# A weight sum made one product ahead in the first down phase of a hybrid recurrent / gMLP / convolutional-FFN block

## The chip, the cores and the metric

The kernel runs on one core of a Trainium2 chip. Its time is the device time of one execution in microseconds; the median of three runs before the change is 2160.91 us (2159.95 to 2163.38). The engines are TensorE (PE in the rows, its weight loads PEld), VectorE (DVE), ScalarE (ACT), GpSimd (POOL) and SyncE (SP, which here only issues transfers). Sixteen DMA engines move data between HBM and the on-chip memory.

## The reference, cut to what matters

The block takes x of 2048 x 1024 floats. A mixer (a gated linear recurrence and a gMLP side by side) is followed by a feed-forward part, each between two RMS norms with a shift, a scale and a gate worked out from c. The change touches the last product of the feed-forward part alone:

```
h = rmsnorm(x, g_ffn_pre) * (1.0 + sc_f) + sh_f
up = causal_depthwise_conv(h @ w_up, ffn_conv_w, ffn_conv_b)
g_ff, v_ff = split(up, 2)
y = (gelu(g_ff) * v_ff) @ w_down          # 2048 x 3072 by 3072 x 1024
x = x + gt_f * rmsnorm(y, g_ffn_post)
```

Everything is float32. The kernel writes each operand of a matmul as a high part (rounded to the type that TensorE reads) and a low part (the rest), and computes high x high + high x low + low x high: three matmuls for one.

## The kernel before, in words

The positions are worked on in two halves of 1024 (C = 0 and C = 1). After the mixer come four phases: up for C = 0, down for C = 0, up for C = 1, down for C = 1. The last two are the second up phase and the second down phase below.

**A down phase** (`down_fast`) computes g @ w_down by a scheme of the Strassen-Winograd kind: the features are halved into even and odd blocks, the positions and the output columns into halves, and seven products of sums of these quarters take the place of eight of plain quarters. The products run in this order, each named by its left operand and its weight: "11" x "11", "s1" x "t1", "s2" x "t2", "s4" x "22", "s3" x "t3", "12" x "21", "22" x "t4". The left sums s1 to s4 were stored in HBM (gsd) during the up phase. The weights t1 = 12 - 11, t2 = 22 - t1, t3 = 22 - 12 and t4 = 21 - t2 are sums of quarters of w_down. In C = 0 they are made and stored in HBM (wsd), in C = 1 they are loaded from there.

A product has six steps (q = 0 to 5) of 24 matmuls of 128 x 512: two feature blocks, four column blocks, three matmuls each (L1155). Its results gather in four PSUM banks, A or B. A step's operands come from `operands` (L1132 to L1150): the left raw tile is loaded (L1139), cast to its high part by ScalarE (L138), and the low part is a difference on VectorE (L143); the weight likewise. A "t" weight in C = 0 goes through `weight_sum` (L1119 to L1130): it loads both summands, subtracts (L1126), splits, and ScalarE's queue stores the sum (L1129). Between steps, `tick` advances background work. In the first down phase this is `h2_next`, which loads the normed input of the second half (L231, L859, L860) and builds the 28 operand tiles of the second up phase.

**Tiles.** All large tiles are 128 x 1024 floats, 512 KB. They come from four pools: "t4" with 36 (operands of the up phase, results, and here some raw tiles), "w" with 8 (high and low parts), "wraw" with 4 (raw weights), "ld" with 3 (raw loads and the results of the up phase, until these are stored). A pool's tile is given again only when every reader of its last use is done, a store of it included. In the first product, steps 0 and 1 (`first`) take raw tiles and parts from "t4"; the others use "w", "wraw" and, in C = 1, "ld".

**Order.** A planner orders the instructions of each engine and each queue when the kernel is built, by the order in the source and its own estimates of time; `high_priority(offset=n)` moves what stands in its block ahead by n instructions, so that loads and splits run ahead of their use. On the chip each engine and each queue works in that fixed order: a load that must wait for its tile holds back every load behind it in SyncE's queue.

Of the kernel before, what the change touches and what calls it, by code (L numbers as in the profile page):

```python
# [10 lines left out]
F32 = mybir.dt.float32  # L11
F32R = mybir.dt.float32r
AF = mybir.ActivationFunctionType
ALU = mybir.AluOpType

P = 128
# [24 lines left out]
def block_kernel(ctx: ExitStack, tc: tile.TileContext, xt, cols, rows, wada, wada_r, win_k, win_s, win_v, wgate, wsp, wout, wup, wdown, out):  # L41
    nc = tc.nc
    const = ctx.enter_context(tc.tile_pool(name="const", bufs=1))
    tp = hp = ctx.enter_context(tc.tile_pool(name="tp", bufs=36))
    wp = ctx.enter_context(tc.tile_pool(name="wp", bufs=8))
    rw = ctx.enter_context(tc.tile_pool(name="rw", bufs=4))
    lp = ctx.enter_context(tc.tile_pool(name="lp", bufs=3))
# [6 lines left out]
    vec, act, pool, pe, sync = nc.vector, nc.scalar, nc.gpsimd, nc.tensor, nc.sync  # L54

    def t4(name):
        return tp.tile([P, 2, 512], F32, tag="t4", name=name)
# [4 lines left out]
    def h4(name):  # L62
        return hp.tile([P, 2, 512], F32R, tag="t4", name=name)
# [37 lines left out]
    def wait(n):  # L101
        for _ in range(n):
            yield
# [32 lines left out]
    def split(hi, lo, src, eng, leng=None):  # L136
        if eng == "act":
            act.copy(out=hi, in_=src)  # L138
        elif eng == "pool":
            pool.tensor_scalar(out=hi, in0=src, scalar1=1.0, scalar2=0.0, op0=ALU.mult, op1=ALU.add)  # L140
        else:
            vec.tensor_copy(out=hi, in_=src)
        (leng or vec).tensor_tensor(out=lo, in0=src, in1=hi.bitcast(F32), op=ALU.subtract)  # L143

    def weight(src, shape, name, eng="act", leng=None, mk=None, ahead=200, mkraw=None):
        with tc.high_priority(offset=ahead):
            raw = mkraw(f"{name}_r") if mkraw else rw.tile(shape, F32, tag="wraw", name=f"{name}_r")
            sync.dma_start(out=raw, in_=src)
            if mk is None:
                hi = wp.tile(shape, F32R, tag="w", name=f"{name}_h")  # L150
                lo = wp.tile(shape, F32R, tag="w", name=f"{name}_l")
            else:
                hi, lo = mk(shape, f"{name}_h"), mk(shape, f"{name}_l")
            split(hi, lo, raw, eng, leng)
        return hi, lo
# [35 lines left out]
    def rms_split(ssum, name, n=512):  # L191
        with tc.high_priority(offset=100):
            shl = y4(f"{name}_hl")
            split(shl[:, 0, :n], shl[:, 1, :n], ssum, "dve")
        return shl
# [358 lines left out]
    def mixer_out(c, late=False):  # L554
        Yt = Y[c]
        O = []
        q = SumSq(f"rp{c}")
        for j in range(4):
            pt = psum(f"o{c}_{j}")
            for b in range(2):  # L560
                wh, wl = weight_once(("o", 2 * j + b), wout[2 * j + b], [P, 8, P], f"wout{c}_{j}_{b}", pool if b else vec)
                for k in range(8):
                    mm3(pt[:, b], (wh[:, k], wl[:, k]), (Yt[k // 2][0][:, k % 2], Yt[k // 2][1][:, k % 2]), k == 0, k == 7)
                tick()
            o = t4(f"oo{c}_{j}")
            with tc.high_priority(offset=60 if late else 0):
                act.copy(out=o, in_=pt)
            q.add(o)
            if late:
                sync.dma_start(out=o2d[c - 2, :, j], in_=o)  # L570
            else:
                O.append(o)
        return O, q
# [233 lines left out]
    for j in range(2):  # L807
        a = t4(f"xc0_{j}")
# [11 lines left out]
    for c in range(1, NC):  # L820
# [8 lines left out]
        if c + 1 < NC:  # L829
            ht = start(h_task(c + 1, False), norm_scale(c, 3))  # L830
            O, q = mixer_out(c - 1)
# [39 lines left out]
    def h2_sums(C, i, get, plain=()):  # L871

        a21 = get(1, i, "21")
        a22 = get(1, i + 2, "22")
        if plain:
            put(C, i, "22", a22)
        else:
            a12 = get(0, i + 2, "12", True)
        yield
        vec.tensor_tensor(out=a22, in0=a22, in1=a21, op=ALU.add)  # L880
        put(C, i, "s1", a22)
        yield
        a11 = get(0, i, "11")
        if plain:
            put(C, i, "11", a11)
        yield
        vec.tensor_tensor(out=a22, in0=a22, in1=a11, op=ALU.subtract)
        put(C, i, "s2", a22)
        yield
        vec.tensor_tensor(out=a11, in0=a11, in1=a21, op=ALU.subtract)  # L890
        put(C, i, "s3", a11)
        yield
        if plain:
            a12 = get(0, i + 2, "12")
            put(C, i, "12", a12)
            yield
        vec.tensor_tensor(out=a12, in0=a12, in1=a22, op=ALU.subtract)
        put(C, i, "s4", a12)
# [9 lines left out]
    def from_x2(C, i):  # L908
        return lambda t, j, o: normed(C, t, j, f"xf{C}{i}{o}")
# [187 lines left out]
    def down_fast(C):  # L1097
# [2 lines left out]

        HT = 512

        def a_src(op, q):
            if op[0] == "s":
                i, h = {"s2": (0, 0), "s3": (0, 1), "s4": (1, 0), "s1": (1, 1)}[op]
                return gsd[C, :, 2 * q:2 * q + 2, i, h]
            i, h = {"11": (0, 0), "12": (1, 0), "22": (1, 1)}[op]
            g = gd[C, :, 4 * q:4 * q + 4, HT * h:HT * h + HT]
            return g.rearrange("p (a b) t -> p a b t", b=2)[:, :, i]

        def w_src(k, q):
            if k[0] == "t":
                i, h = {"t1": (0, 0), "t3": (0, 1), "t4": (1, 0), "t2": (1, 1)}[k]
                w = wsd[2 * q:2 * q + 2, i]
            else:
                i, h = {"11": (0, 0), "12": (0, 1), "21": (1, 0), "22": (1, 1)}[k]
                w = wdown[4 * q:4 * q + 4].rearrange("(a b) p d c -> a b p d c", b=2)[:, i]
            return w.rearrange("a p d c -> p a d c")[:, :, 4 * h:4 * h + 4]

        def weight_sum(k, q, name):  # L1120

            a, b = {"t1": ("12", "11"), "t2": ("22", "t1"), "t3": ("22", "12"), "t4": ("21", "t2")}[k]
            raw, other = [rw.tile([P, 2, 4, P], F32, tag="wraw", name=f"{name}_{x}") for x in "ro"]
            sync.dma_start(out=raw, in_=w_src(a, q))
            sync.dma_start(out=other, in_=w_src(b, q))
            vec.tensor_tensor(out=raw, in0=raw, in1=other, op=ALU.subtract)  # L1126
            hl = [wp.tile([P, 2, 4, P], F32R, tag="w", name=f"{name}_{x}") for x in "hl"]
            split(hl[0], hl[1], raw, "act")
            act.dma_start(out=w_src(k, q), in_=raw)  # L1129
            return hl  # L1130

        def operands(op, k, q):  # L1132
            with tc.high_priority(offset=150):
                n = f"{op}_{q}"
                n = f"{C}{op}_{q}"
                first = op == "11" and q < 2
                mk = h_like if first else None
                raw = t4(f"dgr{n}") if first or C == 0 else lp.tile([P, 2, 512], F32, tag="ld", name=f"dgr{n}")
                sync.dma_start(out=raw, in_=a_src(op, q))  # L1139
                if C == 0 and not first:  # L1140
                    g = [wp.tile([P, 2, 512], F32R, tag="w", name=f"dg{x}{n}") for x in "hl"]
                else:
                    g = h4(f"dgh{n}"), h4(f"dgl{n}")
                split(g[0], g[1], raw, "act")
                mkraw = (lambda m: tp.tile([P, 2, 4, P], F32, tag="t4", name=m)) if first else None
                if C == 0 and k[0] == "t":
                    w = weight_sum(k, q, f"dw{n}")
                else:
                    w = weight(w_src(k, q), [P, 2, 4, P], f"dw{n}", ahead=0, mkraw=mkraw, mk=mk)
            return g, w  # L1150

        def mm(pt, g, w, a, d, first, stop):
# [91 lines left out]
        hl = rms_split(acc[1], "fr11")  # L1244
# [27 lines left out]
    def h2_next():  # L1272

        for i in range(2):
            yield from wait(4)
            g = h2_sums(1, i, from_x2(1, i), True)
            for _ in g:
                yield from wait(2)
# [5 lines left out]
    O, q = mixer_out(NC - 2, True)  # L1284
# [13 lines left out]
    up_phase(0, PLAIN, lambda f: start(late_chunks()) if f == PLAIN + 1 else None)  # L1298
    drain()
    start(h2_next())  # L1300
    down_fast(0)
    drain()
    up_phase(1, 0, lambda f: start(first_finals()) if f == 1 else None)
    drain()
    down_fast(1)
    drain()

# [69 lines left out]
```

## Time and profile before

| | |
|---|---|
| median of three runs | 2160.91 us |
| the profiled execution, its own time | 2167.42 us |
| its span, first to last instruction | 2165.6 us |
| TensorE busy | 2014.3 us (93%) |
| VectorE busy | 1553.9 us (72%) |
| ScalarE busy | 953.6 us (44%) |
| GpSimd busy | 440.0 us (20%) |
| moved by DMA | 572.46 MB, mean 264 GB/s |
| first down phase | 1170.8 to 1435.7 us |
| second down phase | 1895.7 to 2141.0 us |

Matmuls overlap: one lasts 0.39 us in the rows, and the next starts 0.23 us after it. A stretch in which TensorE is busy throughout is therefore the measure, not the sum of durations. The granted clock is the share of TensorE's 2.4 GHz that the chip gave over a stretch; it has two levels, full and half. A row of busy time by stretch gives the stretch, its length, then for PE, PEld, DVE, ACT and POOL the busy us and the instructions, then the granted clock, the busy share of the DMA engines and their GB/s. A row with [t <- X] says that the engine stood idle for t us before the instruction, and that X ended the wait.

### The profile page before, as it was taken

What the parts mean: (1) busy time and instruction counts of PE and PEld (TensorE: products, weight loads), DVE (VectorE), ACT (ScalarE), POOL (GpSimd) and SP (SyncE); (2) the same over time, 40 slices, a digit from 0 to 9 for tenths busy, and PEclk for the clock granted to TensorE, in tenths of its full rate; (3) what the DMA queues carried; (4) which work ended last, traced back from release to release, by engine and by line L of the source; (5) the groups of instructions that cost most, each with busy time, mean ns of one, the idle gap of its engine ahead of it and who ended that gap; (6) DMA issues with size and microseconds to landing.
All of it is one profiled execution on the core that took longest, in us unless ns stands there. A gap on an engine that the chain in (4) does not pass through costs nothing.

```text
span 2165.6 us, 23968 instructions
## 1 busy us (share of the span) xinstructions
PE 2014.3 (93%) x8744; PEld 1649.3 (76%) x8744; DVE 1553.9 (72%) x1727; ACT 953.6 (44%) x1226; POOL 440.0 (20%) x250
## 2 busy tenths in 40 slices
PE   5898979999998999999998989999999999979995
PEld 3686868878877887787776777788888888868884
DVE  6787698697576698998897867665555776554557
ACT  3463642633644554454554544443323333343432
POOL 3355243333212234425331000020000000000000
PEclk9898989999999999999999999999999999999997
DMA  8487578677585579889787888867776997666545
GB/s 323 165 311 274 194 261 288 241 261 280 188 300 205 222 284 336 318 321 352 268 314 275 318 301 286 285 237 272 271 280 233 342 358 277 220 203 214 194 148 154
DMA packets 198823, 572.46 MB, mean 264 GB/s; under 512 B 17456, under 2 KB 17584, under 8 KB 198704
## 3 DMA queue, kind: packets, MB, share of 16 engines
q1 hardware_dynamic: 183568, 527.93, 68.5%
q0 software_dynamic: 7456, 26.22, 3.3%
q10 hardware_dynamic: 7680, 16.78, 2.0%
q8 instruction: 69, 1.13, 0.2%
q14 instruction: 50, 0.41, 0.1%
HBM read 372.67 MB, written 199.23 MB: 264 GB/s over the span
## 4 chain that ended last, share of the span: by engine, by line
PE 62%; DVE 17%; DMA 10%; issue 5%; ACT 4%; POOL 1%; SPq 0%; DVEq 0%; ACTq 0%; POOLq 0%
PE dA L1155 9%; PE upa L980 6%; PE upa L982 6%; PE upa L981 6%; PE dB L1155 5%; PE upc L980 3%; PE upc L981 3%; PE upc L982 3%; DVE a L929 2%; PE upb L982 1%; PE upb L981 1%; PE upb L980 1%; DMA dw0s_o<-in_wdown_dram 1%; PE lg L179 1%; PE lg L180 1%
## 5 line engine op out<-in xcount | busy, mean ns | idle before, releaser
L929 DVE SCALAR_TENSOR_TENSOR a<-Rg,prm,a 128x1023 f32<-128x1023 f32 x92 | 127.0, 1381 | 72.8 <-ACT a L927 72.7
L929 DVE SCALAR_TENSOR_TENSOR a<-Rv,prm,a 128x1023 f32<-128x1023 f32 x92 | 139.2, 1513 | 20.7 <-ACT a L927 20.3
L960 POOL TENSOR_TENSOR wug<-wuv,wug 128x512 f32<-128x512 f32 x24 | 46.9, 1954 | 506.5 <-DMA wsd<-dw_r 285.5
L1090 POOL DMA_DIRECT2D out_dram<-do x2 | 2.5, 1342 | 703.0 <-DVE do L1088 703.0
L927 ACT ACTIVATE a<-Rv,prm 128x1024 f32<-128x1024 f32 x46 | 57.2, 1244 | 142.0 <-DVE Rv L1047 141.9
L138 ACT CAST wt<-wug 128x512 fp32r<-128x512 f32 x72 | 44.7, 621 | 114.2 <-POOL wug L964 51.2
L1155 PE MATMUL dA<-dgh,dw_h 128*128 128x512 f32 x192 | 73.5, 408 | 21.2 <-ACT dw_h L138 21.2
L143 DVE TENSOR_TENSOR wt<-wug,wt 128x512 fp32r<-128x512 f32 x72 | 67.8, 942 | 30.7 <-ACT wt L138 30.5
L985 ACT ACTIVATE a<-a 128x1024 f32<-128x1024 f32 x48 | 50.9, 1060 | 86.8 <-DVE a L934 45.4
L1155 PE MATMUL dA<-dgl,dw_h 128*128 128x512 f32 x192 | 73.5, 403 | 0.2 <-DVE dgl L143 0.2
L1155 PE MATMUL dA<-dgh,dw_l 128*128 128x512 f32 x192 | 68.2, 391 | 0.5 <-DVE dw_l L143 0.5
L280 DVE SCALAR_TENSOR_TENSOR ada_m<-wada,cact,ada_m 128x1024 f32<-128x1024 f32 x28 | 45.1, 1612 | 29.2 <-DMA wada<-in_wada_r_dram 29.2
L143 DVE TENSOR_TENSOR dw_l<-dw_r,dw_h 128x1024 fp32r<-128x1024 f32 x36 | 43.9, 1220 | 29.0 <-ACT dw_h L138 28.8
L988 DVE TENSOR_TENSOR gg<-a,a 128x1024 f32<-128x1024 f32 x48 | 58.4, 1216 | 5.8 <-ACT a L985 5.7
L143 DVE TENSOR_TENSOR dgl<-dgr,dgh 128x1024 fp32r<-128x1024 f32 x36 | 43.9, 1222 | 24.5 <-ACT dgh L138 24.2
L1155 PEld LDWEIGHTS dA<-dgh,dw_h 128*128 128x128 f32 x192 | 37.5, 196 | 31.4 <-ACT dw_h L138 23.7
L138 ACT CAST dgh<-dgr 128x1024 fp32r<-128x1024 f32 x36 | 37.7, 1047 | 53.0 <-DMA dgr<-gd 22.6
L143 DVE TENSOR_TENSOR dw1s_l<-dw1s_r,dw1s_h 128x1024 fp32r<-128x1024 f32 x24 | 29.3, 1222 | 42.4 <-ACT dw1s_h L138 42.4
L927 ACT ACTIVATE a<-Rg,prm 128x1024 f32<-128x1024 f32 x46 | 57.1, 1242 | 1.2
L138 ACT CAST dw_h<-dw_r 128x1024 fp32r<-128x1024 f32 x36 | 37.7, 1047 | 39.7 <-PE dA L1155 12.2
L222 POOL TENSOR_TENSOR rp_s<-rp_s,rp_s 128x1024 f32<-128x1024 f32 x12 | 31.3, 2606 | 117.0 <-ACT rp_s L218 116.8
L1051 ACT COPY Rg<-upa 128x512 f32<-128x512 f32 x46 | 26.8, 583 | 55.9 <-PE upa L982 55.9
(651 smaller groups left out, 6885.4 us busy)
## 6 DMA issues: line engine op xcount, KB each, us to landing
wkd<-wt SPq DMA_DIRECT2D x88, 512.0 KB, 3.8
wkd<-w SPq DMA_DIRECT2D x66, 512.0 KB, 5.0
w<-wkd SPq DMA_DIRECT2D x66, 512.0 KB, 4.3
gd<-gg SPq DMA_DIRECT2D x48, 512.0 KB, 5.5
gsd<-gg SPq DMA_DIRECT2D x48, 512.0 KB, 4.1
wrt<-wkd SPq DMA_DIRECT2D x44, 512.0 KB, 4.4
wt<-wkd SPq DMA_DIRECT2D x44, 512.0 KB, 4.9
dgr<-gd SPq DMA_DIRECT2D x36, 512.0 KB, 5.0
```

The lines of the kernel that those rows point to most:

```text
L138: act.copy(out=hi, in_=src)
L143: (leng or vec).tensor_tensor(out=lo, in0=src, in1=hi.bitcast(F32), op=ALU.subtract)
L280: vec.scalar_tensor_tensor(out=flat, in0=w, scalar=cact[:, kt:kt + 1], in1=flat, op0=ALU.mult, op1=ALU.add)
L927: act.activation(out=a, in_=R, func=AF.Identity, scale=w[2], bias=col("ffn_conv_b", blk))
L929: vec.scalar_tensor_tensor(out=a[:, s:], in0=R[:, :FT - s], scalar=w[t], in1=a[:, s:], op0=ALU.mult, op1=ALU.add)
L960: pool.tensor_tensor(out=b11, in0=b12, in1=b11, op=ALU.subtract)
L980: pe.matmul(out=pt, lhsT=wh, rhs=mh, start=first and not more and k == 0, stop=False, skip_group_check=more)
L981: pe.matmul(out=pt, lhsT=wh, rhs=ml, start=False, stop=False, skip_group_check=more)
L982: pe.matmul(out=pt, lhsT=wl, rhs=mh, start=False, stop=last and k == 3, skip_group_check=more)
L985: act.activation(out=g, in_=g, func=AF.Gelu_apprx_tanh)
L988: vec.tensor_tensor(out=flat, in0=g, in1=v, op=ALU.mult)
L1155: pe.matmul(out=pt, lhsT=x[:, a, d], rhs=y[:, a], start=first and z == 0, stop=stop and z == 2, skip_group_check=True)
```

## The change

In the first down phase a weight sum is no longer made in the step that uses it. `AHEAD` names, for four products, the sum that is made while they run: t1 in "11", t2 in "s1", t4 in "s2", t3 in "s4". One of the two summands is the raw weight that the product loads for itself anyway. The new `made` loads the other one into a tile of "t4", subtracts on VectorE, and GpSimd's queue stores the result to wsd. A "t" weight is then loaded from wsd like any other weight, in both halves. Second, the first two steps of both down phases lose their tiles of "t4": the left raw tile comes from "wraw" (C = 0) or "ld" (C = 1), the raw weight from "wraw", the parts of the weight from "w", and in C = 0 those of the left operand too. Third, the background work of the first down phase starts four ticks later.

```diff
+        AHEAD = {"11": [("t1", "12", False)], "s1": [("t2", "22", False)], "s2": [("t4", "21", False)], "s4": [("t3", "12", True)]}
...
-        def weight_sum(k, q, name):
-
-            a, b = {"t1": ("12", "11"), "t2": ("22", "t1"), "t3": ("22", "12"), "t4": ("21", "t2")}[k]
-            raw, other = [rw.tile([P, 2, 4, P], F32, tag="wraw", name=f"{name}_{x}") for x in "ro"]
-            sync.dma_start(out=raw, in_=w_src(a, q))
-            sync.dma_start(out=other, in_=w_src(b, q))
-            vec.tensor_tensor(out=raw, in0=raw, in1=other, op=ALU.subtract)
-            hl = [wp.tile([P, 2, 4, P], F32R, tag="w", name=f"{name}_{x}") for x in "hl"]
-            split(hl[0], hl[1], raw, "act")
-            act.dma_start(out=w_src(k, q), in_=raw)
-            return hl
+        def made(src, q, key, raw, first, name):
+
+            load, store = (a_src, a_src) if key[0] == "s" else (w_src, w_src)
+            other = tp.tile(list(raw.shape), F32, tag="t4", name=name)
+            sync.dma_start(out=other, in_=load(src, q))
+            a, b = (raw, other) if first else (other, raw)
+            vec.tensor_tensor(out=other, in0=a, in1=b, op=ALU.subtract)
+            pool.dma_start(out=store(key, q), in_=other)
 
         def operands(op, k, q):
             with tc.high_priority(offset=150):
-                n = f"{op}_{q}"
                 n = f"{C}{op}_{q}"
-                first = op == "11" and q < 2
-                mk = h_like if first else None
-                raw = t4(f"dgr{n}") if first or C == 0 else lp.tile([P, 2, 512], F32, tag="ld", name=f"dgr{n}")
+                if C == 0:
+                    raw = (rw.tile([P, 2, 512], F32, tag="wraw", name=f"dgr{n}") if op == "11" and q < 2 else t4(f"dgr{n}"))
+                else:
+                    raw = lp.tile([P, 2, 512], F32, tag="ld", name=f"dgr{n}")
                 sync.dma_start(out=raw, in_=a_src(op, q))
-                if C == 0 and not first:
+                if C == 0:
                     g = [wp.tile([P, 2, 512], F32R, tag="w", name=f"dg{x}{n}") for x in "hl"]
                 else:
                     g = h4(f"dgh{n}"), h4(f"dgl{n}")
                 split(g[0], g[1], raw, "act")
-                mkraw = (lambda m: tp.tile([P, 2, 4, P], F32, tag="t4", name=m)) if first else None
-                if C == 0 and k[0] == "t":
-                    w = weight_sum(k, q, f"dw{n}")
-                else:
-                    w = weight(w_src(k, q), [P, 2, 4, P], f"dw{n}", ahead=0, mkraw=mkraw, mk=mk)
+                wraw = rw.tile([P, 2, 4, P], F32, tag="wraw", name=f"dwr{n}")
+                w = weight(w_src(k, q), [P, 2, 4, P], f"dw{n}", ahead=0, mkraw=lambda m: wraw)
+            if C == 0 and op in AHEAD:
+                with tc.high_priority(offset=100):
+                    for key, src, first in AHEAD[op]:
+                        made(src, q, key, raw if key[0] == "s" else wraw, first, f"mk{key}_{q}")
             return g, w
...
     def h2_next():
 
         for i in range(2):
-            yield from wait(4)
+            yield from wait(4 if i else 8)
             g = h2_sums(1, i, from_x2(1, i), True)
```

## Rows read from the trace of the kernel before

**Rows 1.** The page's first part: busy us, share of the span, instructions.

```profile
PE 2014.3 (93%) x8744; PEld 1649.3 (76%) x8744; DVE 1553.9 (72%) x1727; ACT 953.6 (44%) x1226; POOL 440.0 (20%) x250
```

**Rows 2.** Busy time by stretch, second down phase: products 1, 2.

```profile
1895.70:1943.90 48.20, 36.35 (x146) 29.38 (x146) 24.54 (x25) 17.99 (x20) 0.00 (x0) 0.89 0.65 211
1943.90:1976.60 32.70, 32.70 (x146) 27.11 (x145) 14.34 (x12) 14.31 (x18) 0.00 (x0) 1.00 0.58 193
```

**Rows 3.** The same view, first down phase: products 1 to 7 in order.

```profile
1170.80:1214.20 43.40, 34.95 (x145) 28.20 (x146) 34.41 (x34) 24.38 (x30) 0.00 (x0) 0.92 0.72 245
1214.20:1251.20 37.00, 34.86 (x146) 28.01 (x145) 27.32 (x25) 19.97 (x25) 0.00 (x0) 0.95 0.91 325
1251.20:1294.80 43.60, 37.20 (x144) 29.43 (x143) 26.42 (x24) 18.79 (x23) 0.00 (x0) 0.88 0.85 303
1294.80:1327.70 32.90, 32.90 (x146) 27.05 (x144) 22.29 (x20) 16.14 (x18) 0.00 (x0) 1.00 0.77 257
1327.70:1366.80 39.10, 35.08 (x145) 28.09 (x145) 31.53 (x32) 19.07 (x23) 0.00 (x0) 0.96 0.90 315
1366.80:1400.60 33.80, 33.05 (x146) 27.06 (x145) 21.37 (x22) 14.32 (x17) 0.00 (x0) 1.00 0.79 276
1400.60:1435.70 35.10, 33.52 (x146) 26.81 (x145) 23.17 (x25) 15.33 (x21) 3.30 (x3) 1.00 0.90 310
```

**Rows 4.** Waits, 1165 to 1445 us: who for whom, us in total, times, longest.

```profile
ACT dw0s_h L138 <- DVE dw0s_r L1126: 22.3, 11, 4.1
DVE dw0s_r L1126 <- DMA dw0s_o<-in_wdown_dram: 10.8, 7, 2.9
```

**Rows 5.** Timeline of TensorE, first down phase: the two longest of its waits.

```profile
1177.46 0.80 PE L1155 MATMUL dA<-dgh,dw_h 128*128 128x512 f32 x1 [6.67 <-ACT dw_h L138]
...
1281.78 0.80 PE L1155 MATMUL dA<-dgh0s,dw0s_h 128*128 128x512 f32 x1 [4.08 <-ACT dw0s_h L138]
```

**Rows 6.** Waits of SyncE's queue, 1165 to 1445 us.

```profile
SPq L148 <- DMA wsd<-dw0s_r: 15.5, 4, 6.4
```

**Rows 7.** DMA issues by line: count, KB each, median us to landing; and L1129.

```profile
wsd<-dw0s_r ACTq DMA_DIRECT2D x18, 512.0 KB, 6.2
...
dgr<-gd SPq DMA_DIRECT2D x36, 512.0 KB, 5.0
...
kept_s<-win_l POOLq DMA_DIRECT2D x12, 512.0 KB, 7.4
...
L1129 ACTq DMA_DIRECT2D wsd<-dw0s_r x18: 366/418/467, 1201.7 to 1359.5; - x18
```

**Rows 8.** Groups of instructions, 1165 to 1445 us: busy us, mean ns | idle before.

```profile
L1126 DVE TENSOR_TENSOR dw0s_r<-dw0s_r,dw0s_o 128x1024 f32<-128x1024 f32 x18 | 22.0, 1223 | 20.8 <-DMA dw0s_o<-in_wdown_dram 10.8 <-DMA dw0s_o<-wsd 7.0 <-issue 3.0
...
L138 ACT CAST dgh<-dgr 128x1024 fp32r<-128x1024 f32 x18 | 18.9, 1048 | 37.3 <-PE dB L1155 11.8 <-DVE dw_r L1126 11.1 <-PE dA L1155 7.4
...
L859 DVE SCALAR_TENSOR_TENSOR xf<-xf,sf,rq_r 128x512 f32<-128x512 f32 x16 | 11.3, 747 | 4.5 <-DMA xf<-x2d 4.5
```

**Rows 9.** Busy time by stretch: two with high DMA rates, and the first down phase.

```profile
600.00:620.00 20.00, 20.00 (x90) 16.57 (x89) 18.20 (x16) 8.82 (x10) 5.03 (x2) 1.00 1.03 405
...
1700.00:1800.00 100.00, 100.00 (x442) 82.82 (x442) 73.06 (x96) 34.35 (x41) 0.00 (x0) 1.00 0.97 356
...
1170.80:1435.70 264.90, 241.55 (x1009) 194.65 (x1010) 186.51 (x180) 127.98 (x149) 3.30 (x3) 0.95 0.83 290
```

**Rows 10.** Timelines of TensorE, SyncE's queue, its waits: start of the second down phase.

```profile
1904.10 0.80 PE L1155 MATMUL dA<-dgh,dw_h 128*128 128x512 f32 x1 [8.24 <-ACT dw_h L138]
...
1915.19 0.79 PE L1155 MATMUL dA<-dgh,dw_h 128*128 128x512 f32 x1 [3.60 <-ACT dw_h L138]
...
1897.99 0.36 SPq L148 DMA_DIRECT2D dw1s_r<-wsd  x1
1898.40 0.47 SPq L148 DMA_DIRECT2D dw_r<-in_wdown_dram  x1
...
SPq L148 <- DVE dw_l L143: 13.7, 4, 5.0
```

## The prediction

> **What bounds the kernel now.** I read the busy shares first: TensorE is busy for 93% of the span, every other engine less [rows 1]. So a gain can only come from stretches in which TensorE stands still or runs at its lower clock. Then I cut the two down phases into their products (windows). A product is 144 matmuls on one pair of operands, six steps of 24. In the second phase the second product takes 32.7 us with TensorE never idle [rows 2]; that is the price of a product with nothing in its way, 5.45 us a step. Set against it, the seven products of the first down phase take 43.4, 37.0, 43.6, 32.9, 39.1, 33.8 and 35.1 us [rows 3]: 36.0 us too much in all. The first product of the second phase takes 48.2 us [rows 2], 15.5 us too much. The rest of the second phase has no such loss. The change can therefore give back at most 36.0 + 15.5 = 51.5 us.
>
> What the reader is to see in rows 3: the slow products are those whose weight is a sum, "t1", "t2", "t3", "t4" (37.0, 43.6, 39.1, 35.1 us), and the first one, which starts after the up phase. The two plain ones in between, 32.9 and 33.8 us, lose almost nothing. The granted clock is 0.88 in the worst product and 1.00 in the plain ones, so each stall is paid a second time: the matmuls behind it run at the lower of the two levels (1.2 GHz in place of 2.4).
>
> The waits say what is late in a sum product. ScalarE waits 22.3 us for the difference before it can make the high part of the weight [rows 4], VectorE waits 10.8 us for one of the two summands [rows 4], and TensorE stands, in the worst case 4.08 us, until that high part is there [rows 5]. SyncE's queue waits 15.5 us until the stored sum has left its buffer [rows 6]: both summands come from a pool of four, and the sum keeps its buffer until its store has landed, 6.2 us more [rows 7]. With two tiles a step, only two steps are in flight.
>
> **The change, part by part.**
>
> *The sum leaves the path of its user.* A "t" step of the first phase now loads a finished weight, as a plain step does. The chain load, difference, cast, matmul loses the difference (1.22 us [rows 8]) and the wait for the second summand. In the four-tile pool a step takes one tile in place of two, and no store holds it, so weights can be loaded four steps ahead. By the plain products the four sum products would then cost 32.9 to 33.8 us, and of their excess of 24.0 us (4.3 + 10.9 + 6.4 + 2.4) some 20 to 24 would go, if nothing came in its place.
>
> *The same work moves one product earlier.* Nothing is saved in total: still 24 differences of 1.22 us on VectorE, 24 second operands and 24 stores. But the loads and stores now stand in products 1 to 4 ("11", "s1", "s2", "s4"), four 512 KB transfers a step, while products 5 to 7 keep two. Before, it was products 2, 3, 5 and 7 that had four. VectorE's count first: 3 x 1.22 = 3.7 us a step, and the background that prepares the next up phase adds 16 multiplications of 0.75 [rows 8], 14 low parts and 8 sums of 1.22 us, 39 us over its 28 steps or 1.4 a step. That is 5.1 of 5.45 us. VectorE takes its work in order, so a difference that waits for its second operand holds back the low parts behind it, and TensorE waits for those. Only 0.35 us a step is spare.
>
> DMA next. Four products move 24 x 4 x 0.524 = 50.3 MB, the background 4.2 MB more, and some 2.1 MB is loaded before the start: 52.4 MB. To fit in 4 x 32.7 = 131 us this needs 400 GB/s. The trace reached 405 over 20 us and 356 over the best stretch of 100 us [rows 9]; the sum products of this stage ran at 303 to 325 [rows 3]. So the bounds for the four products are 131 us (400 GB/s) and 181 us (290 GB/s, about the mean of this phase). I take 147 us, 356 GB/s, from the nearest row in which TensorE was busy throughout and the transfers were as large. That leaves 16 us of the excess of the first four products, which is 26.1 us now (10.7 + 4.3 + 10.9 + 0.2). Gain there: 10 us, with ends of 26 and -24.
>
> The Trainium skill, in "DMA: Bandwidth & Descriptors", section "Where 436 GB/s comes from", says that for transfers between HBM and SBUF the HBM side binds at about 358 GB/s. The trace of 405 GB/s over 20 us does not agree; the 356 over 100 us does not contradict it. An estimate by that page would put the four products at 52.4 / 0.358 = 146 us, and the gain at 11 us; by the row of 405 GB/s it would be 26.
>
> *Products 5 to 7* have two transfers a step and no difference. They take 3 x 33 = 99 us by the plain rows, against 39.1 + 33.8 + 35.1 = 108.0 now. Gain 9, with ends of 10 (nothing left) and 3 (some of the output's work was the cause, and it stays).
>
> *The stores move from ScalarE's queue to GpSimd's.* ScalarE is spared 24 issues of about 0.42 us [rows 7], which gains nothing, since it is busy for only 41 to 56% of each product [rows 3]. GpSimd does nothing in products 1 to 6 [rows 3], so a store that waits there for its difference holds back no other work. SyncE's queue issues the second operands among the other loads, some 0.4 us each [rows 10], three a step and so 1.2 of 5.45 us. A store from GpSimd landed after 7.4 us [rows 7] against 6.2 from ScalarE. The sum is loaded again one product (33 us) after it is made, less four steps of loading ahead (22 us): 11 us, of which the store takes 7. That hides it; if it did not, SyncE's queue would stand, and every load behind it with that.
>
> *The first steps use the common raw tiles.* In the second phase the first two steps took their raw tiles and parts from the big pool, which the up phase still fills. TensorE stands 8.24 and then 3.60 us, each time for the high part of the weight [rows 10]. That cast waited for a load issued at 1898.40 us, when TensorE had already run dry; ahead of it in the queue stood the load of a weight for the second product, which waited for its buffer [rows 10]. With common tiles the first weights take the places that those of later steps take now, and are loaded in the order of use. What is late next is the first operand: its raw tile now comes from a pool of three in which the last two results of the up phase still sit, so that loads go one at a time, about 5.0 [rows 7] + 1.05 + 1.22 [rows 8] = 7.3 us against a step of 5.45, for two or three steps. I count 48.2 -> 37 us: a gain of 11. Ends: 15.5 (all of it) and -6 (the stalls stay, and three steps of 1.9 us come on top).
>
> In the first phase the same edit touches the first transition, where TensorE stands 6.67 us [rows 5]; there the operands' parts also go to the common pool of eight, which holds two steps. This is within the 10 us of the first four products. The later start of the background (four steps) costs nothing: it ends in the sixth product, still before the up phase that needs it.
>
> **Sum.** 10 + 9 + 11 = 30 us. The profiled execution took 2167.4 us, so 2137.4 of its kind; the median of the runs is 6.5 us lower, 2160.9, which gives 2131 us. Nothing left of any stall would be 2109.
>
> **Rivals.**
>
> *A. The stall moves to VectorE.* The difference waits for its operand in VectorE's queue, and the low part of the current weight behind it. For it: the waits of 10.8 us and the like [rows 4], and the 0.35 us that VectorE has to spare a step. Against it: the second operand now has a tile of the big pool and can be asked for early. If the 24 differences each cost TensorE 1 us, with the lower clock behind it, the first four products keep all their 26 us; products 5 to 7 and half of the second transition remain, 9 + 5 = 14 us: 2147.
>
> *B. Slower: the crowded stretch is bound by DMA.* Place: products 1 to 4 of the first phase; price: 52.4 MB at the rate the phase has now, 290 GB/s, are 181 us in place of 156.9, a loss of 24, and products 5 to 7 give back 9. With the three-tile pool of the second phase giving nothing, the kernel ends 15 us later: 2176; with 5 of its gain, 2171. It decides from a rate of 52.4 / (264.9 - 99) = 316 GB/s downward, or 296 if the second transition brings its 11 us. For it: 303 to 325 [rows 3] are near that point. Against it: in those rows the engines also waited on each other, and 405 shows more to be had.
>
> *C. The change does not act as told.* The stored sum is not back in time, SyncE stands for it, and the sum products stay as they are; only the second transition gains, and the extra traffic early takes that again: about 2158 to 2163. Against it: the 11 us of slack, and a store from GpSimd that is only 1.2 us slower in the rows. The Trainium skill, in "SBUF — State Buffer", section "SBUF: two separate sides", warns that the descriptors of a DMA issued from GpSimd wait while VectorE runs an operation in a 2-port mode, as a float copy does; the operations of VectorE here mostly have two tensors as inputs, and no row here shows such a wait.
>
> **How the numbers follow.** The forecast 0.60, A 0.22, C 0.06, B 0.12. The likeliest gives 2131, with its own range of 2113 to 2143. The 8 in 10 must take in A and part of C, and the floor of 2109 is hardly reached: 2113 to 2161. A measurement of this kernel can tell 0.2%, 4.3 us, from no change. Faster by more: the forecast, A and a little of C, 0.83; within: most of C, 0.05; slower: B, 0.12.
>
> **What would show it.** Right: the four sum products at 33 to 34 us once they load finished weights, except where they make the next sum; the rate over the first four products between 340 and 400 GB/s; the windows of products 5 to 7 at 33 us with a granted clock of 1.00; the gap before the second down phase under 3 us. Wrong: a low part of the weight as the releaser of TensorE in products 1 to 4 (A); a rate under 316 GB/s there with ScalarE waiting for loads (B); SyncE's queue waiting for the stores of the sums (C); first steps of the second phase that wait for the raw operand longer than now.

## The result and the profile after

The changed kernel takes 2139.21 us (median of four runs, 2137.91 to 2140.90), the kernel before 2162.14 us beside it (four runs): 22.9 us less, a ratio of 0.9886 with a 95% interval of 0.9871 to 0.9900. Forecast were 2131 us and a range of 2113 to 2161. The profiled execution took 2139.98 us (span 2138.2), 27.4 us less than the one of before; some 3 us of that lie ahead of the first down phase, where nothing is changed, and are the difference of two executions. So the sums below are made on the phases.

The first group is busy time by stretch for the seven products of the first down phase, which answers to [rows 3] (columns as there). The planner now starts product 1 before the up phase is over: 24 matmuls of the up phase, 5.4 us, lie in its stretch.

```profile
1162.10:1208.50 46.40, 40.35 (x169) 32.27 (x167) 33.73 (x33) 19.47 (x25) 4.61 (x7) 0.96 0.94 351
1208.50:1248.50 40.00, 35.22 (x145) 28.61 (x146) 32.63 (x30) 19.02 (x23) 5.68 (x8) 0.91 1.04 391
1248.50:1281.40 32.90, 32.90 (x146) 26.95 (x145) 27.71 (x27) 18.95 (x24) 3.16 (x5) 1.00 1.04 385
1281.40:1314.00 32.60, 32.60 (x145) 27.01 (x144) 25.73 (x25) 18.16 (x22) 4.12 (x6) 1.00 1.05 398
1314.00:1348.00 34.00, 33.30 (x146) 26.83 (x145) 26.47 (x29) 18.24 (x22) 0.00 (x0) 1.00 0.61 213
1348.00:1380.80 32.80, 32.80 (x146) 26.94 (x145) 23.05 (x24) 17.02 (x20) 0.00 (x0) 1.00 0.65 226
1380.80:1413.40 32.60, 32.60 (x145) 27.00 (x144) 17.64 (x20) 14.46 (x20) 3.31 (x3) 1.00 0.54 186
...
1170.80:1314.00 143.20, 132.37 (x563) 107.66 (x562) 113.25 (x107) 72.25 (x86) 17.57 (x24) 0.96 1.03 389
```

Products 3 to 7 now run like plain ones. Products 1 to 4 take 151.9 - 5.4 = 146.5 us (before 156.9), products 5 to 7 99.4 (before 108.0). The last row is the crowded stretch as a whole: 389 GB/s over 143 us, 55.7 MB. What is left stands in products 1 and 2, 41.0 and 40.0 us against 32.7. TensorE's waits there, answering to [rows 5], with what went before the one of 4.73 us:

```profile
1181.81 1.20 PE L1155 MATMUL dA<-dgh,dw_h 128*128 128x512 f32 x4 [3.20 <-ACT dw_h L138]
...
1208.55 0.50 PE L1155 MATMUL dB<-dgh0s,dw0s_h 128*128 128x512 f32 x1 [2.46 <-ACT dw0s_h L138]
...
1206.06 0.33 SPq L1003 DMA_DIRECT2D gsd<-gg  x1
...
1207.85 5.71 SPq L148 DMA_DIRECT2D dwr0s<-wsd  x3
1213.64 1.56 SPq L231 DMA_DIRECT2D xf<-x2d  x2
...
1222.05 2.75 DVE L859 SCALAR_TENSOR_TENSOR xf<-xf,sf,rq_r 128x512 f32<-128x512 f32 x4 [4.45 <-DMA xf<-x2d]
...
1222.83 1.39 ACT L860 ACTIVATE xf<-xf,modc 128x512 f32<-128x512 f32 x2 [6.68 <-DVE xf L859]
...
1228.81 1.04 ACT L138 CAST dw0s_h<-dwr0s 128x1024 fp32r<-128x1024 f32 x1
...
1229.90 0.79 PE L1155 MATMUL dB<-dgh0s,dw0s_h 128*128 128x512 f32 x1 [4.73 <-ACT dw0s_h L138]
```

Read from the bottom: TensorE waits for a cast that ScalarE makes at 1228.81. ScalarE had stood 6.68 us for the background (L860), which waited for VectorE (L859), which stood 4.45 us for the background's load (xf). That load was issued at 1213.64, behind three weight loads in SyncE's queue. Before these the queue had stood 10.6 us, until 1206.06, for a store of the up phase (L1003), whose tile VectorE had yet to finish (L1001; the wait is the row of L1003 in the next fence). No run changes that alone, so its share in the stop stays open. The weight itself is not late; the work in front of it is. The waits of the sums in [rows 4] and [rows 6] are gone or small: no row of VectorE waiting for a second operand is left among the longest, and SyncE's queue waits 2.9 us for the stores of the sums.

```profile
ACT xf L860 <- DVE xf L859: 8.8, 2, 6.7
...
SPq L1003 <- DVE gg L1001: 11.9, 2, 10.6
...
SPq L148 <- DMA wsd<-mkt: 2.9, 2, 2.0
```

The second down phase, answering to [rows 2] and [rows 10]: product 1 takes 43.1 us in place of 48.2. The second stop of 3.60 us is gone, the first has only changed its releaser: it now ends with the left operand, no longer with the weight.

```profile
1873.50:1916.60 43.10, 35.12 (x146) 28.81 (x146) 24.45 (x25) 17.95 (x20) 0.00 (x0) 0.88 0.71 244
```

```profile
1869.77 6.31 SPq L148 DMA_DIRECT2D dwr1s<-wsd  x2
1876.17 0.42 SPq L1138 DMA_DIRECT2D dgr<-gd  x1
...
1878.39 1.06 ACT L985 ACTIVATE a<-a 128x1024 f32<-128x1024 f32 x1 [2.95 <-DVE a L934]
1880.43 1.05 ACT L138 CAST dgh<-dgr 128x1024 fp32r<-128x1024 f32 x1 [0.98 <-DMA dgr<-gd]
...
1881.53 2.08 PE L1155 MATMUL dA<-dgh,dw_h 128*128 128x512 f32 x4 [7.98 <-ACT dgh L138]
```

The first left operand is loaded at 1876.17 us, 2.6 us after TensorE ran dry, behind two loads of weights of product 2 (dwr1s) that waited for their tiles: what happened to the first weight in [rows 10] now happens to the left operand. But ScalarE stood only 0.98 us for that load. Until 1879.45 it had the last results of the up phase in front of the cast (L985), and for these it stood 2.95 us for VectorE. Before the change it was the same, with 1.27 us for the load of the weight:

```profile
1900.67 1.06 ACT L985 ACTIVATE a<-a 128x1024 f32<-128x1024 f32 x1 [1.99 <-DVE a L934]
1903.00 1.04 ACT L138 CAST dw_h<-dw_r 128x1024 fp32r<-128x1024 f32 x1 [1.27 <-DMA dw_r<-in_wdown_dram]
```

### The profile page after: what moved, and what is told of

Its sections match the earlier page's. It is cut to its first block, busy times and chain, and to the rows that moved or that the text cites. A ratio compares the mean times of both kernels' runs of the same rounds, so it can differ in the third digit from the quotient of the medians.

```text
span 2138.2 us, 24026 instructions
## 1 busy us (share of the span) xinstructions
PE 2006.5 (94%) x8744; PEld 1645.3 (77%) x8744; DVE 1552.7 (73%) x1727; ACT 951.7 (45%) x1226; POOL 457.9 (21%) x274
## 3 DMA queue, kind: packets, MB, share of 16 engines
q10 hardware_dynamic: 1152, 4.19, 0.5%
## 4 chain that ended last, share of the span: by engine, by line
PE 69%; DVE 16%; DMA 5%; issue 5%; ACT 4%; POOL 1%; SPq 0%; DVEq 0%; ACTq 0%; POOLq 0%
PE dA L1155 11%; PE dB L1155 8%; PE upa L980 6%; PE upa L982 6%; PE upa L981 6%; PE upc L981 3%; PE upc L980 3%; PE upc L982 3%; DVE a L929 2%; PE upb L981 1%; PE upb L982 1%; PE upb L980 1%; PE lg L179 1%; PE lg L180 1%; PE lg L181 1%
## 5 line engine op out<-in xcount | busy, mean ns | idle before, releaser
L929 DVE SCALAR_TENSOR_TENSOR a<-Rg,prm,a 128x1023 f32<-128x1023 f32 x92 | 127.0, 1380 | 69.2 <-ACT a L927 69.1
L929 DVE SCALAR_TENSOR_TENSOR a<-Rv,prm,a 128x1023 f32<-128x1023 f32 x92 | 139.2, 1513 | 20.9 <-ACT a L927 20.6
L927 ACT ACTIVATE a<-Rv,prm 128x1024 f32<-128x1024 f32 x46 | 57.2, 1244 | 140.7 <-DVE Rv L1047 140.6
L985 ACT ACTIVATE a<-a 128x1024 f32<-128x1024 f32 x48 | 50.9, 1061 | 88.9 <-DVE a L934 45.4
L1155 PE MATMUL dA<-dgh,dw_h 128*128 128x512 f32 x192 | 69.7, 396 | 11.2 <-ACT dgh L138 8.0
L143 DVE TENSOR_TENSOR dw_l<-dwr,dw_h 128x1024 fp32r<-128x1024 f32 x36 | 43.9, 1220 | 24.7 <-ACT dw_h L138 24.1
L927 ACT ACTIVATE a<-Rg,prm 128x1024 f32<-128x1024 f32 x46 | 57.2, 1242 | 1.3
L143 DVE TENSOR_TENSOR dw1s_l<-dwr1s,dw1s_h 128x1024 fp32r<-128x1024 f32 x24 | 29.3, 1222 | 38.2 <-ACT dw1s_h L138 38.2
L138 ACT CAST dw_h<-dwr 128x1024 fp32r<-128x1024 f32 x36 | 37.8, 1050 | 37.1 <-PE dB L1155 8.7
L1051 ACT COPY Rg<-upa 128x512 f32<-128x512 f32 x46 | 26.9, 584 | 52.5 <-PE upa L982 52.5
```

What stands on the lines that cost most here:

```text
L927: act.activation(out=a, in_=R, func=AF.Identity, scale=w[2], bias=col("ffn_conv_b", blk))
L929: vec.scalar_tensor_tensor(out=a[:, s:], in0=R[:, :FT - s], scalar=w[t], in1=a[:, s:], op0=ALU.mult, op1=ALU.add)
L985: act.activation(out=g, in_=g, func=AF.Gelu_apprx_tanh)
L1155: pe.matmul(out=pt, lhsT=x[:, a, d], rhs=y[:, a], start=first and z == 0, stop=stop and z == 2, skip_group_check=True)
```

## The experiments

Two theories were open after the result. D: in products 1 to 4 the DMA engines are full, and TensorE pays for the bytes. W: the engines and queues stand in their fixed order for other work, the background above all. And the change has three parts, sums ahead (S), first tiles (T) and the later background (B), whose shares a single pair of kernels can't tell. Each ratio below is against the kernel before in the same batch, with its 95% interval. The cuts of code are against the change, in e2 against the kernel before; `...` marks what is left out.

**e1: S and B without T.** The two first steps of product 1 keep their tiles of the big pool, in both halves:

```diff
-                if C == 0:
-                    raw = (rw.tile(...) if op == "11" and q < 2 else t4(f"dgr{n}"))
+                first = op == "11" and q < 2
+                mk = h_like if first else None
+                if C == 0 or first:
+                    raw = t4(f"dgr{n}")
...
-                wraw = rw.tile([P, 2, 4, P], F32, tag="wraw", name=f"dwr{n}")
+                wraw = (tp.tile(...) if first else rw.tile(...))
...
```

> The sums are made one product ahead as in the change, but the first two steps of product 1 keep their tiles of the big pool in both down phases. Theory (the two parts add up: the sums bring about 19 us in the first down phase, the tiles about 5 us at the start of the second): about 2144 us, 18 us under before, and the start of the second down phase stands some 8 and 3.6 us as before. Rival (the tiles also shorten the start of the first down phase, and the sums alone lose there): over 2150.

2155.76 us, ratio 0.9951 (0.9936 to 0.9965). The rival holds: beside the two other parts T is worth 16.6 us in the medians, 14 by the ratios, not 5. The profile shows where: product 1 of the first phase takes 51.9 us, with stops of 6.67 and 7.27 us, and the second phase starts as before (8.41 and 3.25 us). In every kernel here with T the planner starts product 1 before the up phase is over, and the first of these stops is 3.2 us or gone; in the two without T, this one and the kernel before, it starts behind the up phase and stands 6.67.

```profile
1174.98 0.80 PE L1157 MATMUL dA<-dgh,dw_h 128*128 128x512 f32 x1 [6.67 <-ACT dw_h L138]
...
1188.23 1.04 ACT L138 CAST dw_h<-dwr 128x1024 fp32r<-128x1024 f32 x1 [5.73 <-DMA dwr<-in_wdown_dram]
```

**e2: T alone.** The sums stay in `weight_sum`, the background starts after 4 steps.

```diff
-                first = op == "11" and q < 2
-                mk = h_like if first else None
-                raw = t4(f"dgr{n}") if first or C == 0 else lp.tile(...)
+                if C == 0:
+                    raw = (rw.tile(...) if op == "11" and q < 2 else t4(f"dgr{n}"))
+                else:
+                    raw = lp.tile(...)
...
-                    w = weight(w_src(k, q), [P, 2, 4, P], f"dw{n}", ahead=0, mkraw=mkraw, mk=mk)
+                    w = weight(w_src(k, q), [P, 2, 4, P], f"dw{n}", ahead=0)
```

> The first two steps use the common raw tiles in both down phases, the sums stay in the step that uses them, the background starts as before. Theory (parts add up): about 2156 us, 5 us under before, with the sum products at 37 to 43 us as before. Rival (the tiles were what the sums needed; alone they bring nothing or tie up the four raw tiles): 2162 or more.

2165.36 us, ratio 1.0000 (0.9989 to 1.0012): nothing, as the rival said. The second phase gains its 5 us (43.2 us), the first loses 8: one stop of 16.95 us in product 1. Its chain ends as that of the 4.73 us above does: ScalarE stands 17.74 us for the background.

```profile
1203.33 2.74 DVE L859 SCALAR_TENSOR_TENSOR xf<-xf,sf,rq_r 128x512 f32<-128x512 f32 x4 [6.59 <-DMA xf<-x2d]
...
1204.11 1.38 ACT L860 ACTIVATE xf<-xf,modc 128x512 f32<-128x512 f32 x2 [17.74 <-DVE xf L859]
```

**e8: S and T without B.**

```diff
-            yield from wait(4 if i else 8)
+            yield from wait(4)
```

> The change without its third part: the background starts after 4 steps, as before. Theory (the later start is what keeps its loads out of product 1, where ScalarE and VectorE stand in order for them): 5 to 10 us slower than the change, 2144 to 2149. Rival (it matters little where in the full stretch those 4.2 MB lie): 2138 to 2141.

2148.77 us, ratio 0.9929 (0.9905 to 0.9954), 9.6 us over the change's 2139.21. The theory holds. The stop is in product 1, 10.94 us, and the rows are those of W again. The load of the background is issued at 1199.56. In front of it stand three weights that waited 7.6 us for the stores of their sums, and two stores of the up phase's results; for the first of these to land it waited 3.0 us, as both take their tiles from the pool of three (the two rows of the queue's waits, 1180 to 1201 us).

```profile
1185.45 8.30 SPq L148 DMA_DIRECT2D dwr0s<-wsd  x3
...
SPq L148 <- DMA wsd<-mkt: 7.6, 3, 3.7
SPq L231 <- DMA gsd<-gg: 3.7, 2, 3.0
...
1199.56 1.59 SPq L231 DMA_DIRECT2D xf<-x2d  x2
...
1203.50 1.42 DVE L859 SCALAR_TENSOR_TENSOR xf<-xf,sf,rq_r 128x512 f32<-128x512 f32 x2 [7.35 <-DMA xf<-x2d]
...
1204.29 1.38 ACT L860 ACTIVATE xf<-xf,modc 128x512 f32<-128x512 f32 x2 [11.13 <-DVE xf L859]
```

**e9: T and B without S**, which is e2 with

```diff
-            yield from wait(4)
+            yield from wait(4 if i else 8)
```

> The sums stay in the step that uses them; the first steps use the common raw tiles and the background starts after 8 steps in its first half, as in the change. With the tiles alone the first down phase lost 8 us, in one stop of 16.95 us while ScalarE stood for a late load of the background. Theory (that stop is the background's early loads; the later start removes it, the sum products stay slow): 8 to 13 us under the tiles alone, 2152 to 2157. Rival (two summands a step in a pool of four that also holds two left tiles is the cause): 2160 to 2166.

2146.76 us, ratio 0.9931 (0.9912 to 0.9950): the theory in kind, but more than it said, 18.6 us under T alone where 8 to 13 were expected. Beside the change in its own batch (e12) the sums bring 2146.76 - 2140.31 = 6.5 us. Its products show what the sums give and take:

```profile
1159.10:1197.80 38.70, 38.39 (x169) 31.45 (x168) 29.10 (x29) 19.16 (x23) 0.00 (x0) 1.00 0.76 275
1197.80:1236.20 38.40, 33.75 (x146) 26.66 (x144) 30.53 (x29) 22.15 (x28) 0.00 (x0) 1.00 0.98 339
1236.20:1279.40 43.20, 36.28 (x144) 28.77 (x145) 27.78 (x26) 18.71 (x22) 0.00 (x0) 0.92 0.90 313
...
1312.10:1351.60 39.50, 35.31 (x146) 27.85 (x145) 32.71 (x34) 19.54 (x23) 0.00 (x0) 0.96 0.88 311
```

Without the sums ahead, product 1 takes 38.7 - 5.4 = 33.3 us, nearly nothing lost; products 2, 3 and 5 are slow as ever (38.4, 43.2, 39.5). The sums ahead take 15.6 us from products 2 to 7 (220.5 to 204.9) and give 7.7 back in product 1 (33.3 to 41.0).

The length of the first down phase (less the 5.4 us where the up phase reaches into it) and of product 1 of the second puts the parts side by side:

| kernel | first down phase, us | second, product 1, us | median, us |
|---|---|---|---|
| before | 264.9 | 48.2 | 2160.9 to 2164.8 by batch |
| T (e2) | 272.7 | 43.2 | 2165.4 |
| S and B (e1) | 253.4 | 48.3 | 2155.8 |
| S and T (e8) | 256.1 | 43.2 | 2148.8 |
| T and B (e9) | 253.7 | 42.7 | 2146.8 |
| S, T and B: the change | 245.9 | 43.1 | 2139.2 |

Leaving out any one part costs 6.5 to 16.6 us; together these are 32.7, more than the whole gain of 22.9, while T alone brings nothing. The parts lean on each other. S alone and B alone were not run.

**e3: the background later still.**

```diff
-            yield from wait(4 if i else 8)
+            yield from wait(1 if i else 17)
```

> The change, with the background of the first down phase started 9 steps later still (17 in place of 8, and 1 in place of 4 before its second half), so that its loads fall into products 3 to 6. Theory W (what is left in product 2 is ScalarE and VectorE standing in order for a late load of the background): the 4.73 us stop in product 2 and the lower clock behind it go, 7 us, about 2132. Theory D (the DMA engines are full in products 1 to 4 and TensorE loses what the bytes take): 1 to 2 loads, 1 MB, leave product 2 and as much comes to products 3 and 4, which stand then; the sum of products 1 to 4 falls by no more than 3 us unless bytes leave the four products: 2136 to 2140.

2139.22 us, ratio 0.9869 (0.9852 to 0.9887): no change, as D said. The stop of 4.73 us leaves product 2, and one of 3.79 us comes at the start of product 3. The stretches of the four products sum to 151.8 us, in the change to 151.9. That speaks against W's price, not against its mechanism: in front of the cast that ends the new stop ScalarE again works for the background (L860 at 1242.61, then a cast of its tile). The rows of products 2 and 3:

```profile
1209.20:1245.90 36.70, 32.91 (x145) 26.93 (x145) 24.12 (x23) 17.63 (x22) 4.11 (x6) 1.00 1.04 392
1245.90:1281.80 35.90, 34.56 (x144) 28.15 (x145) 27.23 (x24) 14.64 (x16) 5.82 (x8) 0.95 1.02 373
```

**e5 and e6: twelve loads more.** Both add loads that nothing reads, e5 to products 3 and 4, e6 to products 6 and 7:

```diff
+            if C == 0 and op in ("s2", "s4"):        # e6: ("12", "22")
+                with tc.high_priority(offset=100):
+                    extra = t4(f"ex{n}")
+                    sync.dma_start(out=extra, in_=a_src("11", q))
             return g, w
```

> The change, with one load of 512 KB more in each step of products 3 and 4 (12 loads, 6.3 MB; nothing reads them). Theory D (the DMA engines are full there, at some 390 GB/s, and TensorE pays for every byte): 6.3 MB / 0.39 = 16 us more, about 2155, with TensorE standing in products 3 to 5. Theory W (what is left of the stall is the engines' order, the transfers are hidden): 0 to 3 us more, 2139 to 2142.

> The same 12 loads more, now in products 6 and 7, where the change moves 226 and 186 GB/s. Both theories: nothing to pay, 2139 to 2141; over 2145 would mean that not the DMA engines but an issue slot or a tile of the big pool is what an extra load costs, and the run before it could not be read.

e5: 2151.62 us, ratio 0.9941 (0.9919 to 0.9964), 12.4 over the change. e6: 2139.49, ratio 0.9884 (0.9860 to 0.9908), nothing. So an issue and a tile more cost nothing by themselves. In e5 the rate does not rise above the change's 385 and 398; the products get longer instead:

```profile
1246.00:1288.20 42.20, 33.16 (x145) 26.65 (x143) 28.90 (x27) 22.48 (x29) 2.92 (x5) 0.94 1.05 395
1288.20:1324.80 36.60, 35.63 (x144) 28.93 (x145) 25.32 (x24) 15.54 (x18) 4.36 (x6) 0.92 1.05 397
```

6.3 MB at 0.39 MB/us are 16 us; 13.3 us of that are paid in these two products (78.8 against 65.5). D holds for what is added there: the stretch has no room left.

**e7: t4 made in product 6.**

```diff
-        AHEAD = {..., "s2": [("t4", "21", False)], "s4": [("t3", "12", True)]}
+        AHEAD = {..., "s4": [("t3", "12", True)], "12": [("t4", "t2", True)]}
```

> The change, with t4 made in product 6 from its weight 21 and the stored t2, in place of product 3: 6.3 MB leave the crowded products 1 to 4. Theory D: products 2 and 3 and their loads ahead get room, some of the 7 us lost in product 2 comes back, 2133 to 2137; no more, because products 1 and 2 keep their own four transfers a step. Theory W: the stop in product 2 stays, 2139.

2138.42 us, ratio 0.9879 (0.9852 to 0.9906): not told from the change; this one goes to W. Product 2 has become less full (347 GB/s, busy share 0.95), and its stop stays, with ScalarE standing 5.54 us for the background (L860) in front of the cast:

```profile
1208.60:1248.50 39.90, 35.63 (x145) 28.91 (x146) 31.81 (x30) 19.07 (x23) 4.14 (x6) 0.91 0.95 347
...
1229.46 0.79 PE L1155 MATMUL dB<-dgh0s,dw0s_h 128*128 128x512 f32 x1 [4.27 <-ACT dw0s_h L138]
```

**e4: the left tile of the second phase from the four raw tiles.**

```diff
-                if C == 0:
-                    raw = (rw.tile(...) if op == "11" and q < 2 else t4(f"dgr{n}"))
+                if op == "11" and q < 2:
+                    raw = rw.tile(...)
+                elif C == 0:
+                    raw = t4(f"dgr{n}")
```

> The change, with the left raw tile of steps 0 and 1 of the second down phase's product 1 taken from the pool of four raw tiles too (after the change it comes from the pool of three). Theory (the 7.98 us before the second down phase are the first left load, which has no tile or stands in SyncE's queue behind a weight of product 2): the stop falls to under 3 us, about 2131. Rival (with two raw tiles gone to left operands the weights come late instead): the stop stays at 6 to 9 us, now for the weight, 2138 to 2140.

2135.05 us, ratio 0.9857 (0.9840 to 0.9875); the interval overlaps that of the change, so the median alone settles nothing. In the trace the stop is 4.19 us in place of 7.98, and product 1 takes 40.0 us in place of 43.1: about half of what the theory wanted. The left operand is loaded in time now (1855.78). Its cast still stands in ScalarE's queue behind results of the up phase (L1051, L927), but no longer behind L985, which now comes after it, at 1880.44. Tile and order changed together here; the 0.98 us that ScalarE stood for the load in the change suggest that the order is the larger part.

```profile
1855.78 0.37 SPq L1140 DMA_DIRECT2D dgr<-gd  x1
...
1874.07 1.24 ACT L927 ACTIVATE a<-Rg,prm 128x1024 f32<-128x1024 f32 x1
1875.21 1.98 ACT L138 CAST dgh<-dgr 128x1024 fp32r<-128x1024 f32 x2
...
1876.29 2.07 PE L1157 MATMUL dA<-dgh,dw_h 128*128 128x512 f32 x4 [4.19 <-ACT dgh L138]
```

**e10: e3, e4 and e7 together** (their three edits).

> The change with the left raw tiles of the second phase's first steps from the four raw tiles, t4 made in product 6, and the background 9 steps later still. Each of the last two alone brought nothing; theory D: together they can, since the background's 4.2 MB now fall where t4's 6.3 MB have gone: product 2 at 36.7 us as with the late background, product 3 at 33; with the 4 us of the raw tiles 2131. Rival (the stops of products 1 and 2 are made before, by their own transfers, and only the raw tiles count): 2135.

2140.47 us, ratio 0.9895 (0.9880 to 0.9910), level with the change. Neither expectation held. Product 1 of the second phase keeps its gain (39.4 us), but the first phase takes 250.0 us: the background, t3 and t4 now all fall into products 3 to 6 (34.3, 33.1, 34.9, 36.7). No version tried here is shown to beat the change.

**e11: the stores from ScalarE's queue.**

```diff
-            pool.dma_start(out=store(key, q), in_=other)
+            act.dma_start(out=store(key, q), in_=other)
```

> The change, with the stores of the sums issued from ScalarE's queue, as before the change, in place of GpSimd's. Theory (ScalarE then stands for the difference that it stores, and the casts behind it with it): 3 to 10 us slower than the change, 2142 to 2149. Rival (the same bytes on the same engines, and ScalarE has room): 2138 to 2141.

2139.59 us, ratio 0.9892 (0.9876 to 0.9907): the rival, no difference. The queue of the stores is not a part of the gain.

**e12: the change again**, beside e9 to e11.

> The change itself, on the chip of these runs: 2139, for comparison with the three others.

2140.31 us, ratio 0.9894 (0.9880 to 0.9909).

## Why the prediction was right, and where it was not

*The sum.* 10 + 9 + 11 = 30 us were forecast; the phases gave 10.4 + 8.6 + 5.1 = 24.1, the medians 22.9. Two terms were as sized, the third was half.

*"The sum leaves the path of its user."* Right. Products 3, 5 and 7 fell to 32.9, 34.0 and 32.6 us once they loaded finished weights; product 2, the fourth with a sum for its weight, did not (40.0). The comparison of e9 and the change gives this part 15.6 us over products 2 to 7.

*"The same work moves one product earlier."* The length was right (147 forecast, 146.5 measured), the working only in part. The rate was 389 GB/s, not 356, and the bytes 55.7 MB, not 52.4. The forecast's bytes at the measured rate are 135 us, the measured bytes at the forecast's rate 156: that the two errors cancel is luck. The stretch is full, as e5 and e6 show. But the 16 us over the plain price were put down to bytes divided by a rate, and for the 7 of them in product 2 that is not so: e7 makes it less full, and it keeps its stop. That e8, with the same bytes in another order, is 9.6 us slower points the same way. For the 8 in product 1 neither is shown. There a difference (L1128) of 1.22 us stands in VectorE's queue between two operations of the up phase (L929); ScalarE waits 3.66 us for the second of these, and its casts come behind that:

```profile
1176.31 1.22 DVE L1128 TENSOR_TENSOR mkt<-mkt,dwr 128x1024 f32<-128x1024 f32 x1
1177.45 1.28 DVE L929 SCALAR_TENSOR_TENSOR a<-Rg,prm,a 128x1022 f32<-128x1022 f32 x1
...
1178.82 1.06 ACT L985 ACTIVATE a<-a 128x1024 f32<-128x1024 f32 x1 [3.66 <-DVE a L929]
...
1180.71 1.04 ACT L138 CAST dw_h<-dwr 128x1024 fp32r<-128x1024 f32 x1
```

That is rival A in kind, a difference that holds up VectorE's queue, at the transition only. How much of the 7.7 us that product 1 lost it makes up was not tested and stays open. Rival A's price, 24 differences of 1 us each, did not come: products 3 and 4 make 12 of them and lose nothing.

*"The later start of the background (four steps) costs nothing"* is true and misses what matters: the later start was taken for a cost to be hidden, and it is worth 9.6 us (e8), a term that the sum put at nothing. I had priced the background by VectorE's time (1.4 us a step) and bytes (4.2 MB). What it costs is a load that SyncE issues behind others that wait, and two engines that stand in order for it. The stop of 16.95 us in e2 is that price at its highest. A row of the kernel before, not among [rows 4], shows that ScalarE stood for the background there too, in shorter waits:

```profile
ACT xf L860 <- DVE xf L859: 12.9, 7, 3.8
```

*"The first steps use the common raw tiles"* is the step that failed: 48.2 to 37 us was counted, 43.1 measured. The working put the first stop of 8.24 us down to a late load, and took it away with that load. But ScalarE had stood only 1.27 us for it; the rest was mostly the up phase's last results, which stand in front of the cast in ScalarE's fixed order and stayed there. So the stop stayed, 7.98 us, with the lower clock behind it (0.88 over the product), where a gap under 3 us was to show that the forecast was right. The forecast named the right successor, the left operand in the pool of three, but priced it as one load after another (1.9 us a step). What came of its late load is 0.98 us at that stop; e4 takes away about half of the stop, with the load in time and the cast ahead of L985. What went is the second stop, 3.60 us. The working also said that the tiles' part in the first phase lies within the 10 us of the four products; e1 shows that without them the sums lose 7.5 us of the first phase again.

*The stores from GpSimd* cost nothing, as forecast: they landed after 7.2 us in the median, against 7.4 in [rows 7], and e11, whose stores from ScalarE landed after 7.2 too, has the same time. (ScalarE's smallest share of a product in [rows 3] is 42%, not 41; nothing hangs on it.) The Trainium skill's warning in "SBUF — State Buffer", section "SBUF: two separate sides", of descriptors that wait for VectorE, shows in no row here.

*Rival B* did not come: its break-even of 316 GB/s was passed by far. *Rival C*: SyncE's queue waits 2.9 us for stored sums in the change, so it is ruled out there. In e8, with 7.6 us, its wait does come, but products 3 and 5 still take 36.6 and 34.1 us in place of 43.6 and 39.1.

## What to carry to other kernels

Before you price work that runs in the background at nothing, look for what its first load stands behind in the queue, and which engines take its operations in order with those of the critical path: here four steps of delay were worth 9.6 us, more than making the sums earlier (6.5). Moving the same bytes into one stretch can pay even if that stretch fills the DMA engines; here twelve further loads in it then cost most of what their bytes take at that rate (13.3 of 16 us), and in a stretch with room nothing. When a load is late, read how long its user stood for it alone, and what else the user has in front of it (here 0.98 of 7.98 us were the load's). Read also what stands before the load in its queue before giving it another buffer: the new buffer can hand the same place to the next operand.

## What the runs showed of the hardware

The DMA engines moved 389 GB/s over 143 us with TensorE busy 92% of the time, and up to 398 in one product. The Trainium skill, in "DMA: Bandwidth & Descriptors", section "Where 436 GB/s comes from", has the HBM side bind at about 358 GB/s; here, with one core at work, it does not. Transfers took longer to land in that stretch: the background's loads 11.2 us in the median. The same loads in the kernel before, whose first down phase ran at 290 GB/s [rows 9], took 7.1 us (the last row, of the kernel before).

```profile
xf<-x2d SPq DMA_DIRECT2D x8, 512.0 KB, 11.2
...
wsd<-mkt POOLq DMA_DIRECT2D x24, 512.0 KB, 7.2
...
xf<-x2d SPq DMA_DIRECT2D x8, 512.0 KB, 7.1
```
